# A third of the weights' low parts made by accumulating transfers in a two-layer hybrid encoder

## The chip, the cores and the metric

The kernel runs on one core of a Trainium2 chip. The metric is the device time of one execution in microseconds, median of the runs; smaller is better.

## What is computed

Two layers of an encoder over 256 tokens of width 1024, in float32. Each layer has three token mixers in parallel (a gated short convolution, a pooling mixer, windowed attention with 16 heads and 4 KV heads), then a SwiGLU feed-forward part:

```python
h = rms_norm(x, g_mix)
b_a, c_a, x_a, u_p, q, k, v, ga, gp, gt = jnp.split(h @ w_in, split_points(), axis=-1)
y_a = short_conv_mixer(b_a, c_a, x_a, conv_w, w_a_out)
y_p = multiscale_pool_mixer(u_p, w_pool, pool_scale)
y_t = windowed_gqa(q, k, v, rel_bias, sink) @ w_attn_out
x = x + (sigmoid(ga) * y_a + sigmoid(gp) * y_p + sigmoid(gt) * y_t) @ w_o
h2 = rms_norm(x, g_ffn)
gate, up = jnp.split(h2 @ w_gu, [D_FF], axis=-1)
x = x + (silu(gate) * up) @ w_down
...
return rms_norm(x, g_final)     # after the second layer
```

The weights of both layers, about 168 MB, are read once.

## The kernel before

**Split matmuls.** TensorE multiplies in a reduced format (float32r). To keep float32 accuracy, each weight block W and each activation X is split into a high part, which is the value rounded to float32r, and a low part, the value minus the high part. A product is then three matmuls: high by high, high by low, low by high (`mm3`, lines 162 to 164). The low part of the weights is used by the third one.

**The weight stream.** The host lays the weights out in the order in which they are used, as 128 x 128 blocks, 16 to a *chunk* (1 MB, 160 chunks). `dma_chunk` loads a chunk into a `raw` tile by a transfer that is issued on SyncE's queue (SP); there are 3 raw buffers, so chunk c goes into the slot of chunk c - 3 and its load waits until both halves of that chunk are converted. `convert` works on a *half-chunk* `hc` of 8 blocks (128 x 1024, 512 KB; 320 in all): ScalarE (ACT) copies raw to `hi`, rounding it (line 135), and VectorE (DVE) subtracts, `lo = raw - hi` (line 136). There are 5 buffers of hi and 5 of lo, so half-chunk h is written where h - 5 was, after TensorE has used that one. `advance` emits loads three chunks and conversions three half-chunks ahead of their use.

**Order.** The program is one stream in the order of the code; a scheduler (Tile) decides from it the order of instructions on each engine, and each engine and each DMA queue works in its order. Transfers of GpSimd (POOL) carry the small things: constants, the bias table `stab`, which POOL builds and stores at the start (`build_bias`), and, per pair of heads, a bias tile read from that table (`load_bias`, 16 transfers of 384 KB, three tiles ahead). POOL also adds up the squares for the norms.

**Stages of a layer.** K and V, then Q (the first 12 half-chunks of the layer, during which the norm's factors, K's split `kk`, the transposes of V `vp` and Q's splits `q` are made), the gates and the convolution with the attention interleaved, the pooling mixer and the output projection; then 11 steps of the feed-forward part, gate and up columns followed by the rows of `w_down`. Half-chunks 0 to 3 are converted ahead of the first layer, in step with the loading of x.

Of the kernel before, what the change touches and what calls it, by code (L numbers as in the profile page):

```python
# [8 lines left out]
F32 = mybir.dt.float32  # L9
F32R = mybir.dt.float32r  # L10
AF = mybir.ActivationFunctionType
ALU = mybir.AluOpType
# [21 lines left out]


def plan_layer(last):
    """Order in which the 128 x 128 weight blocks (matrix, k, n) of a layer are used."""
    out = []

    def inner(mat, ns, nk=KT):  # L40
        for n in ns:
            for k in range(nk):
                out.append((mat, k, n))

    def outer(mat, ns, nk=KT):
        for k in range(nk):
            for n in ns:
                out.append((mat, k, n))

    outer("in", (CK, CK + 1, CV, CV + 1))  # L50
    for q in range(2):
        inner("in", [CQ + 4 * q + j for j in range(4)])
    inner("in", [CGA + n for n in range(8)])
    for n in range(8):
        inner("in", (CC + n, CX + n, CB + n))
    inner("in", (CU, CU + 1))
    inner("a", range(8))
    for n in range(8):
        inner("in", (CGP + n, CGT + n))
        if n % 2 == 1 and n < 7:  # L60
            inner("in", (CU + n + 1, CU + n + 2))
        inner("t", (n,))
        out.extend(("pool", k, n) for k in range(2))
        if n >= 2:
            out.extend(("o", n - 2, m) for m in range(8))
    for j in range(4):
        out.extend(("o", k, m) for k in (6, 7) for m in (2 * j, 2 * j + 1))
    for q in range(NQ):
        ns = (2 * q, 2 * q + 1, FT + 2 * q, FT + 2 * q + 1)
        if q == 0:  # L70
            outer("gu", ns)
        else:
            inner("gu", ns)
        if q >= 1:
            for k in (2 * q - 2, 2 * q - 1):
                out.extend(("down", k, m) for m in range(8))
    ks = (2 * NQ - 2, 2 * NQ - 1)
    if last:
        for k in ks:
            out.extend(("down", k, m) for m in range(8))  # L80
    else:
        for j in range(4):
            out.extend(("down", k, m) for k in ks for m in (2 * j, 2 * j + 1))
    return out
# [6 lines left out]
def trunk(ctx, tc, wst, xT, chp, sinkb, rb, invc, gfin, ident_d, out):  # L91
# [14 lines left out]
        uid[0] += 1  # L106
        return f"{s}{uid[0]}"

# [1 line left out]
    plan = []  # L110
    for l in range(L):
        plan += [(l,) + key for key in plan_layer(l == L - 1)]
# [15 lines left out]
    def convert(hc):  # L128
        c = hc // 2
        raw = raws[c][:, (hc % 2) * HT * P:(hc % 2 + 1) * HT * P]  # L130
        hi = wp.tile([P, HT * P], F32R, name=f"hi{hc}", tag="hi", bufs=5)
        lo = wp.tile([P, HT * P], F32R, name=f"lo{hc}", tag="lo", bufs=5)
        for a, b in (((0, 4), (4, 8)) if hc == 0 else ((0, 8),)):
            s = slice(a * P, b * P)
            S.activation(hi[:, s], raw[:, s], AF.Copy)  # L135
            V.tensor_tensor(lo[:, s], raw[:, s], hi[:, s].bitcast(F32), op=ALU.subtract)  # L136
        his[hc], los[hc] = hi, lo

    def advance(pos):
# [28 lines left out]
    def half(j):  # L168
        return slice(j * T, (j + 1) * T)

# [1 line left out]
    warm = const.tile([P, T], F32R, name="warm")  # L172
    V.memset(warm.bitcast(F32), 0.0)
    epst = const.tile([P, 1], F32, name="epst")
# [16 lines left out]
    V.memset(ones, 1.0)  # L191
    ident = const.tile([P, P], F32, name="ident")
    G.dma_start(ident, ident_d)
    # [0 | I | 0]
    ident2 = const.tile([P, 3 * P], F32R, name="ident2")
    G.memset(ident2.bitcast(F32), 0.0)
    G.tensor_copy(ident2[:, P:2 * P], ident)
# [2 lines left out]
    inv = const.tile([P, 4, 2, 8], F32, name="inv")  # L200
    G.dma_start(inv, invc)

    # kk[kv]: (high parts of K in both halves of the rows, low parts in one half and zeros in the other)
    kk = [[act.tile([P, T], F32R, name=f"kk{v}{i}") for i in range(2)] for v in range(4)]
    for v in range(4):
        V.memset(kk[v][1].bitcast(F32), 0.0)
    ups = [act.tile([P, T + 16], F32, name=f"up{i}") for i in range(2)]
    for u in ups:
        V.memset(u, 0.0)
    # vt[key tile]: per pair of KV heads (a, b) the columns [a high | a low | b low | b high]  # L210
    vt = [act.tile([P, 2, 4, 64], F32R, name=f"vt{kt}") for kt in range(2)]

    stab = dpool.tile([16, 512], F32, name="stab")

    def build_bias():
        """stab[h, i] = rel_bias[bucket(255 - i), h] inside the window, NEG outside."""
        st = tmp.tile([16, 512], F32, name="st", tag="t2", bufs=8)
        G.memset(st, NEG)
        G.tensor_copy(st[:, 248:255], rbt[:, 17:24][:, ::-1])
        G.tensor_copy(st[:, 255:263], rbt[:, 0:8])  # L220
        for i, (a, b) in enumerate(RANGES):
            G.tensor_copy(st[:, 255 - b:256 - a], rbt[:, 24 + i:25 + i].to_broadcast([16, b - a + 1]))
            G.tensor_copy(st[:, 255 + a:256 + b], rbt[:, 8 + i:9 + i].to_broadcast([16, b - a + 1]))
        G.dma_start(stab, st)
# [12 lines left out]
        t = pool.tile([P, 2, T], F32R, name=nm(name), tag=tag, bufs=bufs)  # L237
        return t[:, 0, :], t[:, 1, :]

# [1 line left out]
    def xg_tiles(l, gi, j, st):  # L241
        """x tiles 2j, 2j+1 times the gain, split."""
        for k in (2 * j, 2 * j + 1):
            g = ch[:, l, gi, k:k + 1]
            h, lo = pair(act, "xz", 8, "xg")
            if j < XJ:
                V.tensor_scalar(h, x[:, k], g, None, op0=ALU.mult)  # L247
            else:
                S.activation(h, x[:, k], AF.Copy, scale=g)
            V.scalar_tensor_tensor(lo, x[:, k], g, h.bitcast(F32), op0=ALU.mult, op1=ALU.subtract)  # L250
            st["xg"].append((h, lo))

    def squares(j, st):
        """Squares of x tiles 2j, 2j+1, added up."""
        sq = tmp.tile([P, 2, T], F32, name=nm("sq"), tag="t2", bufs=8)
        S.activation(sq, x[:, 2 * j:2 * j + 2], AF.Square)
        if j == 0:
# [6 lines left out]
            st["sum"] = s1  # L264

    def preload(func, src):
        """Has the activation table of func loaded once src is there."""
        d = tmp.tile([P, 1], F32, name=nm("pre"), tag="pre", bufs=2)
        S.activation(d, src, func)

    def rsqrt(r, sd, ms):
        """r = ms ** -0.5 from the table's square root, one Newton step on top."""
        V.reciprocal(r, sd)
        V.tensor_tensor(ms, ms, r, op=ALU.mult)
        V.tensor_tensor(ms, ms, r, op=ALU.mult)
# [15 lines left out]
        st["q"], st["ps"] = rr, ps  # L291

    def norm_rows(st):
        """The tokens' factors as rows, the same on all partitions."""
        rr, ps = st["q"], st["ps"]
        for i in range(4):
            tb = i % 2
# [38 lines left out]
        for k in range(nk):  # L336
            mm3(dst, (l, mat, k, n), xs[koff + k][0], xs[koff + k][1], start=(k == 0), stop=(k == nk - 1))

# [1 line left out]
    def att_scores(l, t, qs, st):  # L340
        bias = st["bias"].pop(t)
        ss = []
# [53 lines left out]
        split(h, lo, f)  # L396
        st["ao"][t] = (h, lo)

# [1 line left out]
    def t1(name):  # L400
        return tmp.tile([P, T], F32, name=nm(name), tag="t1", bufs=10)

    def mixer(l, st):
        xg = st["xg"]
        def kv_out():
            norm_rows(st)
            r = st["r"]
            # K reversed in the tokens
            for p in range(2):
                kf = t1("kf")  # L410
                V.tensor_tensor(kf[:, ::-1], kb[:, half(p)], r, op=ALU.mult)
# [91 lines left out]
        def pool_mixer(n, bank, j):  # L503
# [7 lines left out]
            for d in (1, 2, 4)[:g]:  # L511
# [1 line left out]
                lo_, hi_ = lo_ + d, hi_ - d  # L513
                V.tensor_tensor(s2[:, lo_:hi_], s[:, lo_ - d:hi_ - d], s[:, lo_ + d:hi_ + d], op=ALU.add)
                s = s2
            # the ends divide by their own counts: the constant is window / count there
            e = bass.AP(tensor=s.tensor, offset=s.offset + 8, ap=[list(s.ap[0]), [T - 8, 2], [1, 8]])
            V.tensor_tensor(e, e, inv[:, g], op=ALU.mult)
            pf = t1("pf")
# [181 lines left out]
    for l in range(L):  # L701
# [13 lines left out]
        else:  # L715
            fms = [tmp.tile([P, 8], F32, name=nm("fm"), tag="sm", bufs=6) for _ in range(2)]

            def sums(tb):
                """fm[0], fm[1]: sums of squares of the halves; fm[2]: the first as a share of the mean, + EPS."""
                fm = fms[tb]  # L720
                for hh in range(2):
                    y = xn[2 * tb + hh]
# [40 lines left out]
MH = 1  # L763
XJ = 1
POOLW = (2, 4, 8, 16)
# distances in the window that share one of the T5 buckets 8..15 (exact buckets below 8)
RANGES = ((8, 11), (12, 15), (16, 22), (23, 31), (32, 45), (46, 63), (64, 90), (91, 128))
SC0, SCD, TRD, PVD = 4, 4.3, 4, 6

# [63 lines left out]
```

## Time and profile before

| | before |
|---|---|
| median of 3 runs | 981.03 us (981.01 to 981.97) |
| profiled execution, span from the first to the last instruction | 980.1 us |
| granted TensorE clock | 0.998 |
| busy: TensorE / VectorE / ScalarE / GpSimd | 968.1 / 715.7 / 554.0 / 45.7 us |
| instructions | 19200 |
| moved by DMA | 178.12 MB, mean 182 GB/s |

The profile gives the profiled execution's span, 980.1 us, and no other time of its own; the median of the runs is 0.9 us above it. The page groups instructions by line and tile and gives for each group the busy time, the mean duration and the idle time of its engine just ahead of it, with what ended that idle time. "PE" is TensorE, "PEld" its weight loads, which overlap its matmuls; a matmul's row in a timeline shows its pipelined duration, and one of 256 columns starts about every 0.12 us. "SPq" and "POOL ... DMA_DIRECT2D" rows are the issues of transfers, and the time "to landing" runs from there to the completion.

### The profile page before, as it was taken

Reading aid. Unit: us, or ns where it says so; the run is one execution under the profiler, and the core shown is the slowest. Engines: PE = TensorE matmul, PEld = TensorE weight load, DVE = VectorE, ACT = ScalarE, POOL = GpSimd, SP = SyncE. Lnnn points to the kernel's source line nnn. Section 1 sums busy time; section 2 is a strip of 40 time slices with the busy share of each in tenths; the row PEclk is TensorE's granted clock in tenths of the full one; section 3 lists DMA queues with packets and bytes.
Section 4 is the critical chain, followed back from the end, with each engine's and each line's share of the span. In section 5 each row is a group of like instructions: output and inputs, shape, how many; then the busy total and the mean of one; then the engine's idle time right before and its main releaser. Section 6 shows DMA issues by size and latency. Waiting matters only on the chain.

```text
span 980.1 us, 19200 instructions
## 1 busy us (share of the span) xinstructions
PE 968.1 (99%) x7877; PEld 954.4 (97%) x7877; DVE 715.7 (73%) x1332; ACT 554.0 (57%) x931; POOL 45.7 (5%) x66
## 2 busy tenths in 40 slices
PE   8999999999999999999999999999999999999996
PEld 7999999999999999999999999999999999999995
DVE  7899898567668955545589898985777697555554
ACT  5866776654456544444477576765554564444443
POOL 5100000000001000000020000000000020000001
PEclk9999999999999999999999999999999999999999
DMA  8755544555554455455443745445554555545531
GB/s 279 254 193 197 189 161 163 197 180 183 189 199 171 174 189 199 173 178 205 178 172 130 248 163 188 161 143 174 192 193 173 172 194 189 200 170 204 184 129 43
DMA packets 27112, 178.12 MB, mean 182 GB/s; under 512 B 3280, under 2 KB 3808, under 8 KB 6800
## 3 DMA queue, kind: packets, MB, share of 16 engines
q1 hardware_dynamic: 24912, 169.93, 49.1%
q0 software_dynamic: 2112, 6.97, 2.5%
q8 instruction: 61, 1.00, 0.4%
q14 instruction: 27, 0.22, 0.1%
HBM read 175.80 MB, written 1.08 MB: 180 GB/s over the span
## 4 chain that ended last, share of the span: by engine, by line
PE 97%; DMA 1%; DVE 1%; SPq 0%; ACT 0%; issue 0%; DVEq 0%; ACTq 0%
PE b L162 25%; PE b L164 25%; PE b L163 25%; PE dn L164 2%; PE dn L162 2%; PE dn L163 2%; PE dn L617 2%; PE dn L616 2%; PE dn L615 2%; PE wo L162 2%; PE wo L163 2%; PE o L389 2%; PE wo L164 2%; PE pt L374 1%; DMA x<-xT 1%; PE sc L348 1%
## 5 line engine op out<-in xcount | busy, mean ns | idle before, releaser
L136 DVE TENSOR_TENSOR lo<-raw,hi 128x1024 fp32r<-128x1024 f32 (+1 forms) x321 | 390.0, 1222 | 215.2 <-ACT hi L135 214.4
L135 ACT ACTIVATE hi<-raw 128x1024 fp32r<-128x1024 f32 (+1 forms) x321 | 337.2, 1055 | 333.1 <-PE b L163 215.0
L162 PE MATMUL b<-h,hi 128*128 128x256 f32 x1344 | 379.8, 283 | 0.0
L164 PE MATMUL b<-h,lo 128*128 128x256 f32 x1344 | 378.4, 282 | 0.0
L163 PE MATMUL b<-h,hi 128*128 128x256 f32 x1344 | 378.3, 281 | 0.0
L162 PEld LDWEIGHTS b<-h,hi 128*128 128x128 f32 x1344 | 253.2, 188 | 0.2
L163 PEld LDWEIGHTS b<-h,hi 128*128 128x128 f32 x1344 | 253.1, 188 | 0.2
L164 PEld LDWEIGHTS b<-h,lo 128*128 128x128 f32 x1344 | 253.1, 188 | 0.0
L163 PE MATMUL b<-xg,hi 128*128 128x256 f32 x448 | 126.6, 283 | 1.6 <-DVE xg L250 1.6
L162 PE MATMUL b<-xg,hi 128*128 128x256 f32 x448 | 126.3, 283 | 1.1 <-DVE xg L247 0.8
L164 PE MATMUL b<-xg,lo 128*128 128x256 f32 x448 | 126.0, 282 | 0.0
L163 PEld LDWEIGHTS b<-xg,hi 128*128 128x128 f32 x448 | 84.4, 188 | 2.3 <-DVE xg L250 2.2
L162 PEld LDWEIGHTS b<-xg,hi 128*128 128x128 f32 x448 | 84.2, 188 | 1.6 <-issue 1.1
L164 PEld LDWEIGHTS b<-xg,lo 128*128 128x128 f32 x448 | 84.4, 188 | 0.0
L164 PE MATMUL dn<-fa,lo 128*128 128x256 f32 x176 | 49.5, 281 | 0.0
L163 PE MATMUL dn<-fa,hi 128*128 128x256 f32 x176 | 49.5, 281 | 0.0
L162 PE MATMUL dn<-fa,hi 128*128 128x256 f32 x176 | 49.5, 281 | 0.0
L260 POOL TENSOR_TENSOR sq<-sq,sq 128x512 f32<-128x512 f32 x12 | 16.2, 1353 | 507.3 <-DVE xg L250 315.5
L358 ACT ACTIVATE s<-s,sm 128x256 f32<-128x256 f32 x64 | 31.8, 500 | 13.0 <-DVE sm L355 13.0
L162 PE MATMUL b<-z,hi 128*128 128x256 f32 x128 | 36.4, 284 | 0.0
L164 PE MATMUL b<-z,lo 128*128 128x256 f32 x128 | 36.1, 282 | 0.0
L164 PE MATMUL b<-ao,lo 128*128 128x256 f32 x128 | 36.0, 282 | 0.0
(174 smaller groups left out, 1537.9 us busy)
## 6 DMA issues: line engine op xcount, KB each, us to landing
raw<-wst SPq DMA_DIRECT2D x158, 1024.0 KB, 4.9
bias<-stab POOLq DMA_DIRECT2D x16, 384.0 KB, 3.9
raw<-wst SPq DMA_DIRECT2D x3, 512.0 KB, 7.7
out<-xn SPq DMA_DIRECT2D x4, 256.0 KB, 2.0
x<-xT SPq DMA_DIRECT2D x3, 256.0 KB, 8.2
raw<-wst SPq DMA_DIRECT2D x2, 256.0 KB, 4.2
gf<-gfin POOLq DMA_DIRECT2D x2, 256.0 KB, 3.8
x<-xT SPq DMA_DIRECT2D x2, 128.0 KB, 4.6
```

The lines of the kernel that those rows point to most:

```text
L135: S.activation(hi[:, s], raw[:, s], AF.Copy)
L136: V.tensor_tensor(lo[:, s], raw[:, s], hi[:, s].bitcast(F32), op=ALU.subtract)
L162: PE.matmul(dst, wh, xh, start=start, stop=False, skip_group_check=skip)
L163: PE.matmul(dst, wh, xl, start=False, stop=False, skip_group_check=skip)
L164: last_mm[0] = PE.matmul(dst, wl, xh, start=False, stop=stop, skip_group_check=skip)
L260: G.tensor_tensor(st["acc"], st["acc"], sq, op=ALU.add)
L348: PE.matmul(ps[:, half(j)], qs[t][j][:, cs], kh, start=True, stop=False)
L358: S.activation(s[:, j], s[:, j], AF.Exp, bias=sm[:, 2 + j:3 + j], accum_out=sm[:, 6 + j:7 + j])
L389: PE.matmul(ps[:, half(j)], vv, pts[kt][i][:, half(j)], start=(kt == i == 0), stop=(kt == i == 1))
L615: PE.matmul(d, ah[:, cs], wh, start=(k == 0), stop=False)
L616: PE.matmul(d, ah[:, cs], wl, start=False, stop=False)
L617: PE.matmul(d, al[:, cs], wh, start=False, stop=(k == FT - 1))
```

## The change

For half-chunks from 8 on whose number leaves 2 when divided by 3 (8, 11, 14, ... 317: 104 of 320), ScalarE writes minus the rounded value into `lo`, a transfer issued by GpSimd then adds `raw` to it in place, and ScalarE makes `hi` by the same copy as before. The subtraction on VectorE is left out for these.

```diff
         hi = wp.tile([P, HT * P], F32R, name=f"hi{hc}", tag="hi", bufs=5)
         lo = wp.tile([P, HT * P], F32R, name=f"lo{hc}", tag="lo", bufs=5)
-        for a, b in (((0, 4), (4, 8)) if hc == 0 else ((0, 8),)):
-            s = slice(a * P, b * P)
-            S.activation(hi[:, s], raw[:, s], AF.Copy)
-            V.tensor_tensor(lo[:, s], raw[:, s], hi[:, s].bitcast(F32), op=ALU.subtract)
+        if hc >= 8 and hc % 3 == 2:
+            S.activation(lo, raw, AF.Copy, scale=-1.0)
+            G.dma_start(lo.bitcast(F32), raw, accum_op=ALU.add)
+            S.activation(hi, raw, AF.Copy)
+        else:
+            for a, b in (((0, 4), (4, 8)) if hc == 0 else ((0, 8),)):
+                s = slice(a * P, b * P)
+                S.activation(hi[:, s], raw[:, s], AF.Copy)
+                V.tensor_tensor(lo[:, s], raw[:, s], hi[:, s].bitcast(F32), op=ALU.subtract)
```

Lines behind the change move down by 5, so L162 to L164 before are L167 to L169 after, and POOL's bias load, L229, is L234. In the rows below a tile's name carries the number of its half-chunk or chunk (`lo8`, `raw4`) and a serial number.

On GpSimd's queue at the start, before: behind the table's store come the three first bias loads, then the next bias load.

```order
L224 DMA stab_151<-st_207 16x512 [waits Pool_49]
L229 DMA bias16_342<-stab_151 128x2x384 [waits DMASW4_49]
L229 DMA bias17_344<-stab_151 128x2x384
L229 DMA bias18_346<-stab_151 128x2x384
L229 DMA bias73_915<-stab_151 128x2x384 [waits DMASW5_49,DVE_49]
```

The same place after:

```order
L229 DMA stab_151<-st_207 16x512 [waits Pool_49]
L234 DMA bias16_342<-stab_151 128x2x384 [waits DMASW4_49]
L234 DMA bias17_344<-stab_151 128x2x384
L234 DMA bias18_346<-stab_151 128x2x384
L135 DMA lo8_397<-raw4_312 128x1024 [waits DMAHW5_49,PE_49,Activation_49]
L135 DMA lo11_548<-raw5_394 128x1024 [waits DVE_49,DMAHW6_49,PE_49,Activation_49]
```

The accumulations of half-chunks 8 and 11, and three more, stand between the third bias load and the fourth. On TensorE the place where half-chunk 8 begins, behind the four transposes of V, after the change (before, the third row has no wait of its own):

```order
L458 MATMUL vp37_540<-ident_124,vf29_449 128x128
L167 MATMUL b38_545<-xg1_158,hi8_396 128x256 [waits Activation_49]
L168 MATMUL b38_545<-xg1_158,hi8_396 128x256
L169 MATMUL b38_545<-xg1_158,lo8_397 128x256 [waits DMASW0_49]
L167 MATMUL b38_545<-xg2_161,hi8_396 128x256
```

The third matmul now waits for the transfer that writes `lo8`. On SP, the load of chunk 7, which goes into the slot of chunk 4, waits for that transfer too (`DMASW0`). ScalarE at the start of the second layer, half-chunks 175 to 177, before:

```order
L135 ACTIVATE hi175_6721<-raw87_6606 128x1024 [waits PE_49,Activation_49]
L233 ACTIVATE h500_6793<-hf499_6791 128x256 [waits DVE_49]
L135 ACTIVATE hi176_6751<-raw88_6664 128x1024 [waits DMAHW1_49,PE_49,Activation_49]
L233 ACTIVATE q491_6709<-qf490_6707 64x256 [waits DVE_49]
L233 ACTIVATE q491_6709<-qf490_6707 64x256
L233 ACTIVATE q492_6715<-qf490_6707 64x256 [waits DVE_49]
L233 ACTIVATE q492_6715<-qf490_6707 64x256
```

and after:

```order
L140 ACTIVATE hi175_6777<-raw87_6661 128x1024 [waits PE_49,Activation_49]
L136 ACTIVATE hi176_6807<-raw88_6720 128x1024 [waits DMAHW1_49,PE_49,Activation_49]
L238 ACTIVATE q491_6765<-qf490_6763 64x256 [waits DVE_49]
L238 ACTIVATE q491_6765<-qf490_6763 64x256
L238 ACTIVATE q492_6771<-qf490_6763 64x256 [waits DVE_49]
L238 ACTIVATE q492_6771<-qf490_6763 64x256
L134 ACTIVATE lo176_6808<-raw88_6720 128x1024 [waits DMASW3_49,PE_49]
```

The copy of minus the high part stands behind the four copies of q; for most other changed half-chunks in the feed-forward part it follows the copy to `hi` directly. TensorE's order is the same apart from a few matmuls of the output projection that change places.

## The prediction

> **What bounds the kernel now.** I read the page first: its busy times, its chain, and the two groups that the change touches.
>
> ```profile
> PE 968.1 (99%) x7877; PEld 954.4 (97%) x7877; DVE 715.7 (73%) x1332; ACT 554.0 (57%) x931; POOL 45.7 (5%) x66
> ...
> PE 97%; DMA 1%; DVE 1%; SPq 0%; ACT 0%; issue 0%; DVEq 0%; ACTq 0%
> ...
> L136 DVE TENSOR_TENSOR lo<-raw,hi 128x1024 fp32r<-128x1024 f32 (+1 forms) x321 | 390.0, 1222 | 215.2 <-ACT hi L135 214.4
> ...
> L135 ACT ACTIVATE hi<-raw 128x1024 fp32r<-128x1024 f32 (+1 forms) x321 | 337.2, 1055 | 333.1 <-PE b L163 215.0 <-PE dn L163 30.7 <-issue 30.2
> ```
>
> TensorE is busy for 968.1 of 980.1 us and is 97% of the chain that ended last. The subtraction that is partly removed is VectorE's largest group, but it is not on the chain. The converter on ScalarE waits for TensorE (215.0 us for the matmuls of line 163): it runs as far ahead as its buffers let it. Next I asked what TensorE itself waits for:
>
> ```profile
> PE b L163 <- DVE xg L250: 1.6, 2, 0.9
> PE wps L180 <- DVE epst L175: 1.2, 1, 1.2
> PE b L162 <- DVE xg L247: 0.8, 1, 0.8
> PE b L162 <- ACT xg L249: 0.3, 1, 0.3
> ```
>
> That is all of it, 3.9 us, and it is the start, when x and the first weights arrive, ahead of half-chunk 8. So a faster VectorE can give nothing that counts, and every wait that the change brings to TensorE adds to the time in full. The question is only where a transfer lands too late.
>
> **The change, part by part.**
>
> *Counts.* Half-chunks 8, 11, ... 317 change, 104 of 320. VectorE loses 104 x 1.222 = 127 us, off the chain: 0. ScalarE gains 104 copies of the same shape as line 135, 104 x 1.055 = 110 us, so 664 of 980 us; the cover is its idle time, the 333.1 us ahead of line 135 for a start. POOL gains 104 transfers of 512 KB, each of which reads two operands (raw and the old lo) and writes lo. TensorE's work is unchanged, and it now waits for a transfer where lo is first used, at the third matmul of the half-chunk.
>
> *One transfer, issue to landing.* No row shows an accumulating transfer or one from SBUF to SBUF. The nearest are POOL's plain loads and the weight loads:
>
> ```profile
> q1 hardware_dynamic: 24912, 169.93, 49.1%
> q0 software_dynamic: 2112, 6.97, 2.5%
> ...
> gf<-gfin POOLq DMA_DIRECT2D x2, 256.0 KB, 3.8
> ```
>
> ```profile
> DMA to landing us min/median/max: 3.6/3.9/8.0
> ```
>
> ```profile
> 33.00:35.00 2.00, 2.00 (x20) 2.00 (x19) 1.96 (x4) 1.94 (x5) 0.27 (x1) 1.00 0.95 311
> ...
> 37.00:39.00 2.00, 2.00 (x20) 2.00 (x19) 1.89 (x6) 1.88 (x6) 0.00 (x0) 1.00 0.66 238
> 39.00:41.00 2.00, 2.00 (x20) 2.00 (x18) 1.97 (x5) 1.95 (x4) 0.00 (x0) 1.00 0.06 22
> ...
> 47.00:50.00 3.00, 3.00 (x27) 3.00 (x27) 2.88 (x7) 2.06 (x4) 0.00 (x0) 1.00 0.99 391
> ```
>
> The second fence is the 16 bias loads, the third the stages of the start (the last two columns are the DMA share and GB/s). Full DMA engines moved 391 GB/s. I count both operands of the accumulation as bytes to move: 2 x 0.524 = 1.05 MB, 2.7 us of all 16 engines. From below it would be one copy, 1.3 us; from above the slow pace of POOL's own queue, 2.5% of 980.1 us for 6.97 MB = 3.5 us per MB, 3.7 us, and beyond that nothing in the trace bounds an adder that is slower than the reads. I take 2.7, since these are long contiguous rows like those of the weight loads. With the 3.8 us of the gain load (0.26 MB) as base: 3.8 + (1.05 - 0.26) MB / 391 GB/s = 5.8 us from issue to landing; ends 3.6 (the fastest POOL transfer) and 8.0 + 2.0 = 10 us.
>
> [...]
>
> *The steady stage: covered, but not by much.* ScalarE and the loads in the FFN:
>
> ```profile
> 399.69 1.06 ACT L135 ACTIVATE hi<-raw 128x1024 fp32r<-128x1024 f32 x1 [1.77 <-PE dn L163]
> 402.55 1.06 ACT L135 ACTIVATE hi<-raw 128x1024 fp32r<-128x1024 f32 x1 [1.80 <-PE b L163]
> ...
> 411.03 1.06 ACT L135 ACTIVATE hi<-raw 128x1024 fp32r<-128x1024 f32 x1 [1.79 <-PE b L163]
> ```
>
> ```profile
> L125 SPq DMA_DIRECT2D raw<-wst x6: 327/328/328, 399.2 to 427.6; - x6
> ...
> DMA to landing us min/median/max: 4.7/4.8/4.9
> ```
>
> A half-chunk takes (411.03 - 399.69) / 4 = 2.84 us. There are five buffers, so a conversion starts when TensorE begins the half-chunk four places earlier: lo is due 4 x 2.84 + 0.24 = 11.6 us later. Two copies on ScalarE take 2.1, which leaves 9.5 us for a transfer of 5.8. Cover 3.7 us. The second reader of the transfer is SP: the weight load into the same raw slot now waits for the accumulation in place of VectorE. The slot is needed again 5 x 2.84 = 14.2 us after its second half began to be converted; 14.2 - 2.1 - 4.8 = 7.3 us for a transfer of 5.8, and a later load only makes ScalarE late, which still has the 3.7 us. The DMA engines go from 49.1 + 2.5 = 51.6% (506 us) to 506 + 104 x 2.7 = 787 us, 80%. I put the steady stage at 0 and name what it rests on: if the engine time were 3.7 us it would be 891 us, 91%, and collisions with the weight loads would show; from (980 - 506) / 104 = 4.6 us on the DMA engines are the bound.
>
> *The first one, half-chunk 8: not covered.* POOL's queue is in order, and the transfer of half-chunk 8 stands behind the three bias loads, which wait for the table:
>
> ```profile
> 26.30 0.51 POOL L224 DMA_DIRECT2D stab<-st  x1 [0.29 <-POOL st L223]
> 31.11 2.16 POOL L229 DMA_DIRECT2D bias<-stab  x3 [4.30 <-DMA stab<-st]
> 66.05 0.71 POOL L229 DMA_DIRECT2D bias<-stab  x1 [32.78 <-DVE sm L356]
> ```
>
> ```profile
> 26.65 1.99 ACT L135 ACTIVATE hi<-raw 128x1024 fp32r<-128x1024 f32 x2
> ```
>
> ```profile
> 33.91 0.60 PE L453 MATMUL vp<-ident,vf 128*128 128x128 f32 x4
> 34.27 0.36 PE L162 MATMUL b<-xg,hi 128*128 128x256 f32 x1
> 34.47 0.27 PE L163 MATMUL b<-xg,hi 128*128 128x256 f32 x1
> 34.59 0.28 PE L164 MATMUL b<-xg,lo 128*128 128x256 f32 x1
> ```
>
> ```profile
> L229 POOL DMA_DIRECT2D bias<-stab x3: 712/716/742, 31.1 to 32.6; - x3
> ...
> DMA to landing us min/median/max: 7.4/7.7/8.0
> ```
>
> ```profile
> L125 SPq DMA_DIRECT2D raw<-wst x3: 328/328/328, 21.9 to 30.1; - x3
> ...
> DMA to landing us min/median/max: 4.9/6.4/6.9
> ```
>
> ScalarE converts half-chunk 8 at 26.65 and has -hi ready by 27.7, but POOL is free only at 31.11 + 2.16 = 33.27. TensorE uses lo 8 right behind the four transposes of V, at 34.59. The transfer would have to land 1.3 us after its issue, and the fastest of POOL took 3.6: at least 36.9 - 34.6 = 2.3 us of wait. The bias loads just ahead of it on the same queue land 7.4 to 8.0 us after their issue, the last by 32.6 + 8.0 = 40.6; with 2.7 us of data behind them lo 8 lands at 43.3, a wait of 8.7. One thing makes this shorter: the weight load issued at 30.1 (chunk 7, into chunk 4's slot) now waits for this very transfer, so the stretch that was 95% full at 33 to 35 us loses 1.05 MB, up to 2.7 us: 6.0. I take the middle, 7.3 us.
>
> [...]
>
> The wait is not given back, since TensorE has no idle time after it. It gives the converters a lead, which covers half-chunk 11, whose copy is ready only at about 40 us where TensorE wants it at 43.5.
>
> *The start of layer 1.* There the scheduler puts the four q copies between the two copies of half-chunk 176:
>
> ```profile
> 529.30 1.06 ACT L135 ACTIVATE hi<-raw 128x1024 fp32r<-128x1024 f32 x1
> 530.26 1.73 ACT L233 ACTIVATE q<-qf 64x256 fp32r<-64x256 f32 x4
> ...
> 540.63 1.06 ACT L135 ACTIVATE hi<-raw 128x1024 fp32r<-128x1024 f32 x1 [1.28 <-PE b L163]
> ```
>
> The last row is the conversion of half-chunk 181, released by the end of 176; so TensorE begins 176 at 540.6 - 2.84 = 537.8 and wants lo at 538.0. The copy of -raw ends at 530.26 + 1.73 + 1.06 = 533.1, plus 5.8 is 538.9: a wait of 0.9 us (from none, if ScalarE is not later, to 2 if it carries the extra copies of 170 and 173 along).
>
> *Queues.* On POOL the later bias loads and the sums of squares may stand behind an accumulation; they are issued with a lead (at 66.05 for a tile three places on), so 0. On SP chunk 7's load waits for lo 8, and those behind it with it; the lead from the wait covers it.
>
> *Sum.* 0 (VectorE) + 0 (ScalarE) + 7.3 (half-chunk 8) + 0.9 (half-chunk 176) + 0 (steady) = 8.2. The profiled span is 980.1, the median of the runs 981.03, 0.9 more, which lies around the span and stays: **989 us**, 0.8% slower.
>
> **The rivals.**
>
> *The stream is overrun (1000 to 1110).* A raw slot whose second half is accumulated goes round once in six half-chunks, 17.0 us: load 4.8, copies of the first half 1.06 and of the second 2.1, transfer 5.8 = 13.8. If in every round the transfer meets a weight load (0.491 x 980.1 us / 169.93 MB x 1.05 MB = 3.0 us) and the load meets a transfer (2.7), it is 19.5, 2.5 too much in each of 53 rounds: 132 us, 1120. Half of that: 1055. For it speaks the thin cover and that nothing bounds the adder from above; against it the 80%. Slower still, with 5.5 us of engine time: 506 + 104 x 5.5 = 1078, plus the start's 33 us: above 1110.
>
> *Not slower (981 to 983).* The same place, half-chunk 8, decides: if its transfer lands within 2.0 us of 34.59, so 3.3 us after its issue, or if the bias table lands a little sooner than the 4.30 us of wait shown and the transfer is as quick as the fastest POOL row (3.6), the wait is under 2 us, and with the rest covered the change is lost in the noise. For it: long rows within SBUF may beat loads; against it: the three landings of 7.4 to 8.0 us just ahead.
>
> *Faster.* Only if VectorE held TensorE somewhere: the 3.9 us of waits all lie ahead of half-chunk 8.
>
> **How the numbers follow.** What a measurement of this kernel can tell from no change is about 0.2%, 2 us. Wait at half-chunk 8 with the steady stage covered: 0.50, between 984 and 1000. Overrun to 1110: 0.31; beyond: 0.12. Not slower: 0.06; faster: 0.01. The range from 984 to 1110 leaves out 0.07 below and 0.12 above; the likeliest case alone spans 984 to 1000. Faster 0.01, same 0.06, slower 0.93.
>
> **What would show it.** In the trace after: TensorE waits once at about 34.6 us for a transfer on lo, 6 to 9 us long; POOL issues it at about 33.3; accumulations land 5 to 7 us after issue in the FFN; ScalarE is busy about 664 us and VectorE about 588; the DMA share is near 80%. Landings above 9.5 us, a wait of TensorE at every third half-chunk, or a DMA share near 95% would show the stream overrun. A wait under 2 us at half-chunk 8 would make the forecast wrong on the other side.

## The result, and the profile after

| | before | after |
|---|---|---|
| median of the runs beside each other | 981.5 us (981.01 to 982.23) | 1026.88 us (1024.33 to 1031.05) |
| ratio, 95% interval | 1 | 1.0466 [1.0451, 1.048] |
| span of the profiled execution | 980.1 us | 1026.8 us |
| granted TensorE clock | 0.998 | 0.985 |

The change makes the kernel 4.7% slower: 45 us where 8 were forecast. One run of e_src below, 1051 us, fell in a slower state of the chip and is left out. The page of the changed kernel, in the parts that were shown of before (busy times, POOL's queue, the chain, the subtraction and the new transfer, its landing):

```profile
PE 982.8 (96%) x7877; PEld 964.9 (94%) x7877; DVE 603.6 (59%) x1228; ACT 649.6 (63%) x1035; POOL 137.2 (13%) x170
...
q0 software_dynamic: 17088, 61.50, 30.4%
...
PE 48%; DMA 31%; issue 12%; DVE 4%; ACT 3%; POOL 2%; SPq 0%; POOLq 0%; ACTq 0%; DVEq 0%
...
L141 DVE TENSOR_TENSOR lo<-raw,hi 128x1024 fp32r<-128x1024 f32 (+1 forms) x217 | 265.1, 1228 | 268.3 <-ACT hi L140 267.9
...
L135 POOL DMA_DIRECT2D lo<-raw x104 | 89.3, 859 | 796.6 <-ACT lo L134 580.2
...
lo<-raw POOLq DMA_DIRECT2D x104, 512.0 KB, 6.1
```

VectorE lost 112 us and ScalarE gained 96, near the counts (127 and 110), but the chain, 97% TensorE before, is now 48% TensorE and 31% DMA. (The chain tells what released what; what TensorE lost stands in its own waits.) What TensorE waits for (us in all, how often, the longest):

```profile
PE b L169 <- DMA lo<-raw: 28.7, 16, 6.9
PE dn L621 <- DMA lo<-raw: 1.8, 1, 1.8
PE b L168 <- DVE xg L255: 1.6, 2, 0.9
PE dn L169 <- DMA lo<-raw: 1.2, 1, 1.2
PE wps L185 <- DVE epst L180: 1.2, 1, 1.2
PE b L167 <- DVE xg L252: 0.7, 1, 0.7
PE wo L169 <- DMA lo<-raw: 0.6, 1, 0.6
```

The rows with `lo<-raw` add up to 32.3 us in 19 waits. The other part stands in the first line of the page: TensorE is busy for 982.8 us instead of 968.1, with the same 7877 instructions, 14.7 us more. 32.3 + 14.7 = 47.0, against a span that grew by 46.7: with these two the account is closed. The longest wait and what follows it, in the timeline of TensorE:

```profile
41.32 0.58 PE L169 MATMUL b<-xg,lo 128*128 128x256 f32 x1 [6.94 <-DMA lo<-raw]
41.70 0.41 PE L167 MATMUL b<-xg,hi 128*128 128x256 f32 x1
41.91 0.41 PE L168 MATMUL b<-xg,hi 128*128 128x256 f32 x1
```

The wait at half-chunk 8 is the one that was forecast. Behind it the matmuls start 0.21 us apart instead of 0.12. The stretches of one microsecond there say why (the column behind POOL's is the granted clock, then the DMA share and GB/s):

```profile
36.00:37.00 1.00, 0.00 (x0) 0.00 (x0) 0.86 (x4) 0.93 (x4) 0.00 (x0) 0.87 1.12 249
37.00:38.00 1.00, 0.00 (x0) 0.00 (x0) 0.97 (x3) 0.99 (x2) 0.00 (x0) 0.50 0.88 177
...
46.00:47.00 1.00, 1.00 (x6) 1.00 (x6) 0.00 (x0) 0.74 (x1) 0.00 (x0) 0.51 1.02 434
47.00:48.00 1.00, 1.00 (x11) 1.00 (x10) 0.65 (x1) 0.63 (x2) 0.00 (x0) 1.00 0.95 401
```

While TensorE idles, its granted clock falls to half, and it is whole again only at 47.0, 5.7 us after the matmuls began again at 41.3: half of 5.7 is 2.8 us lost on top of the wait. Such a stretch follows the waits of 2.10, 2.14, 3.30 and 3.40 us too, and none of 1.78 us or less in this run. The wait of 3.40 us, the time behind it, and the stretch at half clock:

```profile
748.60:752.00 3.40, 0.00 (x2) 0.00 (x1) 0.77 (x1) 1.28 (x2) 0.86 (x1) 1.00 0.94 190
752.00:753.55 1.55, 1.55 (x13) 1.55 (x14) 0.46 (x1) 0.00 (x0) 0.00 (x0) 1.00 1.25 201
753.55:756.96 3.41, 3.41 (x19) 3.41 (x18) 1.88 (x6) 1.72 (x3) 0.00 (x0) 0.50 0.86 327
```

Here the clock is whole all through the wait and falls 1.55 us after TensorE has begun again. The five slow stretches (36.75 to 46.99, then from 330.29, 384.91, 531.68 and 753.55 us on) last 10.2, 3.4, 3.4, 6.8 and 3.4 us. TensorE is busy for 5.67 + 3.42 + 3.21 + 5.98 + 3.41 = 21.7 us of them, so the half clock costs 10.8 of the 14.7 us. The other 3.9 us are about 0.2 us for each of the 19 waits, as in this one, where the overlap of the matmuls (0.28 us long, 0.12 us apart) breaks off:

```profile
237.29 0.28 PE L168 MATMUL b<-h,hi 128*128 128x256 f32 x1
239.12 0.39 PE L169 MATMUL b<-h,lo 128*128 128x256 f32 x1 [1.55 <-DMA lo<-raw]
239.35 0.28 PE L167 MATMUL b<-h,hi 128*128 128x256 f32 x1
```

From the first start to the third it is 2.06 us where two matmuls take 0.24: 1.82 us lost, of which the row's wait has 1.55.

The other 18 waits, 25.4 us, are spread over the run from 239 to 1002 us. Two of them, 2.10 us at 329 (half-chunk 98) and 3.30 at 532 (half-chunk 164), stand behind a norm, where POOL adds up squares. The second one, on ScalarE, on POOL and on TensorE:

```profile
520.11 1.05 ACT L134 ACTIVATE lo<-raw 128x1024 fp32r<-128x1024 f32 x1
```

```profile
517.65 4.17 POOL L265 TENSOR_TENSOR sq<-sq,sq 128x512 f32<-128x512 f32 x3 [6.85 <-ACT sq L261]
521.89 1.60 POOL L268 TENSOR_TENSOR s<-sq 128x256 f32<-128x256 f32 x1
523.45 0.86 POOL L135 DMA_DIRECT2D lo<-raw  x1
```

```profile
532.53 0.58 PE L169 MATMUL b<-xg,lo 128*128 128x256 f32 x1 [3.30 <-DMA lo<-raw]
```

Minus the high part is ready at 520.11 + 1.05 = 521.2, but POOL issues the transfer at 523.45, when its sums are done; TensorE wants lo at 532.53 - 3.30 = 529.2, so only 5.8 us are left for a landing of 9.0. For the other 16, 20.0 us, no other work of POOL stands right ahead of the transfer. One of them in the feed-forward part, from the conversion on ScalarE through POOL's issue and landing to TensorE:

```profile
461.12 1.06 ACT L136 ACTIVATE hi<-raw 128x1024 fp32r<-128x1024 f32 x1 [1.78 <-PE b L168]
```

```profile
463.42 0.86 POOL L135 DMA_DIRECT2D lo<-raw  x1 [7.67 <-ACT lo L134]
```

```profile
474.27 0.39 PE L169 MATMUL b<-h,lo 128*128 128x256 f32 x1 [1.50 <-DMA lo<-raw]
```

```profile
L125 SPq DMA_DIRECT2D raw<-wst x2: 327/355/383, 463.5 to 464.0; - x2
...
DMA to landing us min/median/max: 5.7/8.1/10.4
```

TensorE wanted lo at 474.27 - 1.50 = 472.8, 11.7 us after the conversion began and 9.4 us after the transfer's issue: the lead that was worked out (11.6 and 9.5) is right. The transfer was under way for 10.8 us. The last fence shows two weight loads issued within 0.6 us of it, one of which took 10.4. Over the whole run the 104 transfers and, in the second row, all of SP's weight loads landed so (least, median, most):

```profile
DMA to landing us min/median/max: 4.5/6.1/11.3
...
DMA to landing us min/median/max: 4.7/5.9/11.4
```

The median is inside the lead and the longest is not. Which ones are late can be counted in the trace. Of the 103 transfers behind the first, 19 have no weight load under way 2 us after their issue; they land after 4.5 to 6.4 us, and TensorE waits for none of them. 63 have one load under way (median 6.1, longest 10.4 us) and 21 have two (median 9.6, longest 11.3); all 18 waits are in these two groups. Of the 16 waits, 12, which are 14.5 of the 20.0 us, are for transfers that meet a *pair*: two loads issued within 0.6 us of each other. The pair of the last example began so (SP's waits in the whole run, then the accumulation of half-chunk 143):

```profile
SPq L125 <- DMA lo<-raw: 823.8, 102, 17.1
```

```profile
454.89 0.86 POOL L135 DMA_DIRECT2D lo<-raw  x1 [6.42 <-ACT lo L134]
```

```profile
DMA to landing us min/median/max: 8.5/8.5/8.5
```

An accumulation on the second half of a raw tile (143 is one) holds back the load into that tile's slot. This one landed at 454.89 + 8.51 = 463.4, and the two loads were issued at 463.5 and 464.0. Behind the start there are 19 such pairs, 18 of them begun by a landing, and each met the next transfer, which is on a first half.

Long landings are not the whole of it. At half-chunks 116, 248, 275 and 290 (2.14, 1.32, 1.78 and 0.52 us of wait) the landing took 8.6 to 9.2 us, which a lead of 9.4 covers, but the transfer was issued only 6.5 to 8.5 us ahead of its use. At 116 the weights themselves were late: their load took 8.4 us and landed at 374.05, and ScalarE began the conversion at 374.16.

### The profile page after: what moved, and what is told of

It reads as the page before. It is cut to its first block, busy times and chain, and to the rows that moved or that the text cites. A ratio compares the mean times of both kernels' runs of the same rounds, so it can differ in the third digit from the quotient of the medians.

```text
span 1026.8 us, 19577 instructions
## 1 busy us (share of the span) xinstructions
PE 982.8 (96%) x7877; PEld 964.9 (94%) x7877; DVE 603.6 (59%) x1228; ACT 649.6 (63%) x1035; POOL 137.2 (13%) x170
## 3 DMA queue, kind: packets, MB, share of 16 engines
q0 software_dynamic: 17088, 61.50, 30.4%
## 4 chain that ended last, share of the span: by engine, by line
PE 48%; DMA 31%; issue 12%; DVE 4%; ACT 3%; POOL 2%; SPq 0%; POOLq 0%; ACTq 0%; DVEq 0%
DMA lo<-raw 19%; PE b L169 14%; PE b L167 13%; PE b L168 13%; DMA raw<-wst 11%; PE o L394 1%; PE pt L379 1%; DVE lo L141 1%; ACT hi L140 1%; ACT lo L134 1%; PE sc L354 1%; PE sc L353 1%; PE wo L169 1%; PE wo L167 1%; PE wo L168 1%
## 5 line engine op out<-in xcount | busy, mean ns | idle before, releaser
L141 DVE TENSOR_TENSOR lo<-raw,hi 128x1024 fp32r<-128x1024 f32 (+1 forms) x217 | 265.1, 1228 | 268.3 <-ACT hi L140 267.9
L169 PE MATMUL b<-h,lo 128*128 128x256 f32 x1344 | 380.9, 283 | 16.4 <-DMA lo<-raw 16.3
L167 PE MATMUL b<-h,hi 128*128 128x256 f32 x1344 | 380.4, 283 | 0.0
L140 ACT ACTIVATE hi<-raw 128x1024 fp32r<-128x1024 f32 (+1 forms) x217 | 227.1, 1053 | 189.1 <-PE b L168 96.2
L169 PEld LDWEIGHTS b<-h,lo 128*128 128x128 f32 x1344 | 253.9, 189 | 19.3 <-DMA lo<-raw 19.3
L167 PEld LDWEIGHTS b<-h,hi 128*128 128x128 f32 x1344 | 253.9, 189 | 0.2
L135 POOL DMA_DIRECT2D lo<-raw x104 | 89.3, 859 | 796.6 <-ACT lo L134 580.2
L136 ACT ACTIVATE hi<-raw 128x1024 fp32r<-128x1024 f32 x104 | 109.9, 1057 | 117.7 <-PE b L168 70.3
L169 PE MATMUL b<-xg,lo 128*128 128x256 f32 x448 | 129.6, 290 | 12.4 <-DMA lo<-raw 12.3
L168 PE MATMUL b<-xg,hi 128*128 128x256 f32 x448 | 129.3, 289 | 1.7 <-DVE xg L255 1.6
L167 PE MATMUL b<-xg,hi 128*128 128x256 f32 x448 | 129.3, 290 | 0.7 <-DVE xg L252 0.7
L134 ACT ACTIVATE lo<-raw 128x1024 fp32r<-128x1024 f32 x104 | 108.7, 1045 | 0.1
L169 PEld LDWEIGHTS b<-xg,lo 128*128 128x128 f32 x448 | 87.5, 195 | 13.2 <-DMA lo<-raw 13.2
L168 PEld LDWEIGHTS b<-xg,hi 128*128 128x128 f32 x448 | 87.4, 195 | 2.6 <-DVE xg L255 2.5
L167 PEld LDWEIGHTS b<-xg,hi 128*128 128x128 f32 x448 | 87.5, 196 | 1.0 <-issue 1.0
L169 PE MATMUL dn<-fa,lo 128*128 128x256 f32 x176 | 49.6, 282 | 1.2 <-DMA lo<-raw 1.2
L167 PE MATMUL dn<-fa,hi 128*128 128x256 f32 x176 | 49.5, 281 | 0.0
L169 PE MATMUL wo<-m,lo 128*128 128x256 f32 x128 | 36.1, 282 | 0.6 <-DMA lo<-raw 0.6
L167 PE MATMUL b<-ao,hi 128*128 128x256 f32 x128 | 36.6, 286 | 0.0
```

Source lines behind the costliest of these rows:

```text
L134: S.activation(lo, raw, AF.Copy, scale=-1.0)
L135: G.dma_start(lo.bitcast(F32), raw, accum_op=ALU.add)
L136: S.activation(hi, raw, AF.Copy)
L167: PE.matmul(dst, wh, xh, start=start, stop=False, skip_group_check=skip)
L168: PE.matmul(dst, wh, xl, start=False, stop=False, skip_group_check=skip)
L169: last_mm[0] = PE.matmul(dst, wl, xh, start=False, stop=stop, skip_group_check=skip)
```

## The experiments

The theory after the result (A, in most of the expectations): the change costs by lateness, not by work. The median transfer is covered; those that meet weight loads land after the 9.5 us of lead; each such wait counts in full, and TensorE's half clock behind the longer ones comes on top. The rivals: ScalarE's copies or VectorE's order carry a part; the first wait sets all later ones by taking the lead away; loads held back by the transfers bunch up; or the DMA engines as such are the bound. Eleven kernels, each the changed kernel with the edit shown. "Waits" are TensorE's for the transfer in the profiled execution, "busy" is TensorE's busy time above 968.1 us.

| kernel | transfers | median us (runs) | ratio [95%] | waits us, times | busy + |
|---|---|---|---|---|---|
| after | 104 | 1026.88 (1024.33 to 1031.05) | 1.0466 [1.0451, 1.048] | 32.3, 19 | 14.7 |
| e_act, copies alone | 0 | 982.14 | 1.0005 [0.9995, 1.0014] | none | |
| e_one, half-chunk 8 alone | 1 | 990.58 (990.09 to 990.65) | 1.0088 [1.007, 1.0106] | 6.9, 1 | 1.4 |
| e_warm, the same with 48 matmuls of zeros | 1 | 988.78 (987.78 to 989.63) | 1.0067 [1.0053, 1.0081] | 1.0, 1 | |
| e_from20 | 100 | 1022.02 (1016.28 to 1026.33) | 1.0407 [1.0364, 1.0451] | 23.5, 17 | 10.2 |
| e_even | 52 | 996.2 (995.2 to 997.9) | 1.015 [1.0135, 1.0165] | 9.7, 2 | 3.9 |
| e_even14 | 51 | 988.83 (988.12 to 990.2) | 1.0074 [1.0056, 1.0092] | 5.1, 2 | 2.7 |
| e_odd | 52 | 982.39 | 1.0007 [0.9998, 1.0017] | 0.4, 1 | -0.2 |
| e_lead, one more buffer of lo | 104 | 996.78 (995.45 to 999.99) | 1.0158 [1.0139, 1.0178] | 8.6, 2 | 5.4 |
| e_lead20 | 100 | 992.51 (986.94 to 995.24) | 1.0103 [1.0068, 1.0138] | 4.3, 2 | 0.9 |
| e_copy, plain copies | 104 | 992.67 (991.8 to 994.7) | 1.0115 [1.01, 1.013] | 7.3, 3 | 2.9 |
| e_src, another source | 104 | 1042.23 (1033.5 to 1042.6) | 1.0574 [1.052, 1.0628] | 42.9, 20 | 17.4 |

**The copies without the transfer (e_act).**

```diff
             S.activation(lo, raw, AF.Copy, scale=-1.0)
-            G.dma_start(lo.bitcast(F32), raw, accum_op=ALU.add)
             S.activation(hi, raw, AF.Copy)
+            V.tensor_tensor(lo, raw, hi.bitcast(F32), op=ALU.subtract)
```

> ScalarE makes the extra copies to lo for the 104 half-chunks, but VectorE then subtracts over them as before, and there is no transfer. Theory A (the transfers alone cost time, the 109 us of copies on ScalarE are covered): 981 to 984 us. Rival (the extra copies make ScalarE late in its queue and bring a good part of the waits): above 990 us.

No difference that can be measured. The 104 copies cost ScalarE time that it has, and all of the 45 us belongs to the transfer.

**One transfer alone (e_one).**

```diff
-        if hc >= 8 and hc % 3 == 2:
+        if hc == 8:
```

> Only half-chunk 8 gets its low part by an accumulating transfer; the other 103 keep the subtraction. Theory A (the first transfer stands behind the bias loads, and a TensorE wait of this length is followed by a stretch at half the granted clock): one wait of 6 to 7.5 us at half-chunk 8 as in the changed kernel (6.94), then a granted clock of 0.50 for 5 to 6 us, which costs another 2.5 to 3 us: 981.6 + 6.9 + 2.8 = 991 us (990 to 993), with TensorE busy about 971 us and 0 to 1 us of further waits. Rival 1 (the slow clock costs nothing in the end, or comes only with many transfers): 981.6 + 6.9 = 988.5 us, TensorE busy 968 us. Rival 2 (the first wait is made longer by the next transfers of the queue, at half-chunks 11 and 14): the wait is under 5 us and the time under 988.

The wait is 6.88 us, no different from that with 103 more transfers behind it, so rival 2 is out. In stretches of three microseconds:

```profile
37.00:40.00 3.00, 0.00 (x0) 0.00 (x0) 2.66 (x8) 2.88 (x7) 0.00 (x0) 0.58 0.61 123
40.00:43.00 3.00, 1.54 (x7) 1.55 (x8) 2.97 (x5) 0.22 (x1) 0.00 (x0) 0.50 0.16 26
43.00:46.00 3.00, 3.00 (x22) 3.00 (x22) 0.38 (x1) 0.44 (x1) 0.00 (x0) 0.79 0.95 380
```

In the third row 21% of the clock is missing where half is the only other state seen: 0.42 x 3.00 = 1.3 us at half, so the clock is whole from 44.3 on, 2.8 us after the restart at 41.45. Half of that is 1.4 us, which is what TensorE's busy time rose by. The slow stretch was shorter than the 5 to 6 us expected, and the time, 8.7 us above before, lies at the upper part between rival 1's 6.9 and A's 9.7.

**The same, with TensorE kept busy (e_warm).** Ahead of the matmul that waits, 48 matmuls of zeros, added to the same sum:

```diff
         PE.matmul(dst, wh, xl, start=False, stop=False, skip_group_check=skip)
+        if state["pos"] == 65:
+            for _ in range(48):
+                PE.matmul(dst, warm[:, :P], warm, start=False, stop=False, skip_group_check=skip)
         last_mm[0] = PE.matmul(dst, wl, xh, start=False, stop=stop, skip_group_check=skip)
```

> As the kernel with the one accumulation at half-chunk 8, and TensorE gets 48 matmuls more, of zeros that add nothing to the sum, right ahead of the matmul that waits for that transfer: 48 x 0.12 = 5.8 us of useless work in the place of most of the 6.9 us of idling. Theory A (the half clock behind the wait comes from TensorE's idling and costs time of its own): the granted clock stays 1.00 there, the wait that is left is about 1 us, and the kernel is faster than without the 48 matmuls by what the slow stretch cost, 1.4 us (TensorE busy 969.5 there against 968.1): 989 us against 990.6. Rival (the clock falls for another cause, or the slow stretch is made good later): the same 990.6 us. If the 48 matmuls delayed the transfer, over 992.

```profile
34.37 5.91 PE L171 MATMUL b<-warm 128*128 128x256 f32 x48
41.31 0.39 PE L172 MATMUL b<-xg,lo 128*128 128x256 f32 x1 [1.03 <-DMA lo<-raw]
```

```profile
37.00:40.00 3.00, 3.00 (x28) 3.00 (x26) 2.65 (x8) 2.88 (x7) 0.00 (x0) 1.00 0.83 185
40.00:43.00 3.00, 1.97 (x17) 1.77 (x16) 2.97 (x5) 0.21 (x1) 0.00 (x0) 1.00 0.27 40
```

The transfer lands at the same moment (the third matmul starts at 41.31 against 41.45), the clock stays at 1.00, and the kernel with 48 matmuls more is 1.8 us faster; the runs of the two don't overlap (the intervals of their ratios do, by a little). So the idling of TensorE makes the slow clock behind this wait, and the slow clock costs time of its own.

**The first transfers left out (e_from20).**

```diff
-        if hc >= 8 and hc % 3 == 2:
+        if hc >= 20 and hc % 3 == 2:
```

> The change only from half-chunk 20 on: the four accumulations at the start (8, 11, 14, 17) are subtractions again. Theory A (the wait of 6.9 us at half-chunk 8 is a cost of its own, and the slow clock of about 5.7 us behind it costs another 2.8 us): 1026.9 - 9.7 = 1017 us, first wait gone, the later ones as they are. Rival (that wait only gives the converters a lead which the later accumulations use up; without it they wait earlier or longer): 1023 to 1027 us.

The median is 5 us lower, the profiled run 12, and the runs spread over 10 us: between the two expectations, and it doesn't decide. It does show that the later waits don't need the first one: 17 waits, 23.5 us, are there without it.

**Half of the transfers, twice (e_even, e_odd).** Those on even half-chunks (8, 14, 20, ...), which are the first halves of their raw tiles:

```diff
-        if hc >= 8 and hc % 3 == 2:
+        if hc >= 8 and hc % 6 == 2:
```

> Only half-chunks that leave 2 when divided by 6 (8, 14, 20, ...: 52 accumulations, all on the first half of a chunk). Theory A (late landings come from transfers that meet weight loads released in pairs by an accumulation on a second half): the load of the chunk is no longer released late, later waits go to nothing, about 981 + 6.9 + 2.8 = 991 us. Rival (each accumulation costs the same share whatever its place): half of the 37 us that are not the first wait stay, 981 + 9.7 + 18 = 1009 us.

and those on odd ones (11, 17, 23, ...), the second halves (`hc % 6 == 5`):

> Only half-chunks that leave 5 when divided by 6 (11, 17, ...: 52 accumulations, all on the second half of a chunk, the one whose landing releases the next weight load). Half-chunk 8 is a subtraction, so the first wait is gone unless half-chunk 11 is late. Theory B, the one that is left after the run with the constant source (a transfer is late when it shares the engines with weight loads, whoever releases them; half the transfers leave room): 981 to 988 us. Rival (the place on the second half matters, since its landing holds loads back): 990 to 1005 us.

With 52 odd ones the cost is gone, and TensorE's only wait for a transfer is 0.4 us. Their landings:

```profile
DMA to landing us min/median/max: 4.5/4.6/9.1
```

The median of 4.6 us is next to the least: with twice the distance 45 of the 52 transfers have no weight load under way 2 us after their issue, and the longest, 9.1, is the one behind the wait of 0.4 us. In e_even two waits are left, 5.62 us at half-chunk 8 and 4.04 us at 515 us, half-chunk 164 behind the sums of the norm; none stands in a feed-forward part. Both kernels fit the pairs of loads: without transfers on second halves (e_even) there are 4 pairs instead of 19, and in e_odd there are 11, but no transfer meets one.

**The even ones without half-chunk 8 (e_even14).**

```diff
-        if hc >= 8 and hc % 3 == 2:
+        if hc >= 14 and hc % 6 == 2:
```

> 51 accumulations, at half-chunks 14, 20, 26, ... 314: the kernel with 52 on the even half-chunks without the first one, that at 8. Theory A (what the even ones cost is the first transfer behind the bias loads, and one at the start of the second layer, where a wait of 4.0 us was seen at 515 us): the wait at 40 us is gone, that of 4.0 us stays, and with it 1.5 us of slow clock: 981.6 + 4.0 + 1.5 = 987 us (985 to 989). Rival (a half-chunk in the first half of a raw tile is late in the steady stage too, so that the two waits are a matter of chance in one profile): 990 us or more. If that wait also goes: 982 to 983, equal to the 52 accumulations on odd half-chunks (982.4).

7 us less than e_even, and as A has it a wait stays at the start of the second layer, 3.5 of the 5.1 us. It stands at 508 us, half-chunk 164 again; POOL issues that transfer at 499.3, as soon as its sums are done. The other, 1.6 us at 53 us, was not expected: half-chunk 14 is the first transfer now, and beside two weight loads it took 10.1 us to land. The median is at the upper end of A's range.

**One more buffer of lo (e_lead).** The transfer can start one half-chunk, 2.84 us, sooner against its use (a scratch pool gives up one of ten buffers for the space):

```diff
-        lo = wp.tile([P, HT * P], F32R, name=f"lo{hc}", tag="lo", bufs=5)
+        lo = wp.tile([P, HT * P], F32R, name=f"lo{hc}", tag="lo", bufs=6)
...
-        while state["cv"] < 2 * NCH and state["cv"] * HT <= pos + 3 * HT:
+        while state["cv"] < 2 * NCH and state["cv"] * HT <= pos + 4 * HT:
```

> The changed kernel with 6 instead of 5 buffers of lo and conversions emitted four instead of three half-chunks ahead (the 4 KB come from 9 instead of 10 buffers of a small temporary): a changed half-chunk's copy to lo, and so its transfer, can start one half-chunk, 2.84 us, earlier. Theory A (the later waits are landings of up to 11.3 us against a lead of 9.5 us, and no bound of the DMA engines): all but the first wait go, 981 + 6.9 + 2.8 = 991 us, at most 996. Rival (the DMA engines cannot keep up, so lead is used up): 1010 to 1027 us.

```profile
q0 software_dynamic: 17088, 61.50, 31.3%
```

```profile
DMA to landing us min/median/max: 4.5/7.8/12.2
```

The same bytes in a shorter time, with landings that are later than in the changed kernel (median 7.8 against 6.1), and 30 of the 45 us are gone; of 19 waits two are left, the first of them half-chunk 8. The time is just above A's bound of 996. 26 of the 104 landings are longer than 9.5 us, against 15 in the changed kernel, but the median time from a transfer's issue to TensorE's use of it is 11.7 us instead of 9.4. This is what tells lateness from a bound of the DMA engines: an overloaded engine would not have got faster by a larger buffer.

**Both (e_lead20).** As e_lead, and from half-chunk 20 on.

> The same with the earlier start of conversions, and the change only from half-chunk 20 on: 100 accumulations. Theory A: no wait is left, 981 to 984 us, the time of the kernel before. Rival (DMA engines as the bound): above 1000 us.

The expectation was missed. In the profiled run, the fastest, two waits of 2.0 and 2.3 us are left, but the median lies 5.6 us above it, and what the other runs waited for was not recorded. It didn't beat the kernel before, and no other kernel did.

**A plain copy in the place of the accumulation (e_copy).** lo then holds raw itself.

```diff
-            G.dma_start(lo.bitcast(F32), raw, accum_op=ALU.add)
+            G.dma_start(lo.bitcast(F32), raw)
```

> The 104 transfers are plain copies of raw into lo, same size, same queue, same waits, without the addition (lo is then raw itself; the addition is left out of the result). Theory (the addition costs the second read: 2.77 us of all 16 engines per transfer in the changed kernel): 1.3 to 1.5 us per transfer, landings of about 3.5 us alone, DMA share of about 65%, later waits mostly gone, 985 to 995 us. Rival (the write or the queue sets the pace, the addition is free): 2.5 us or more per transfer, 1015 to 1027 us.

```profile
q0 software_dynamic: 17088, 61.50, 16.3%
...
L135 POOL DMA_DIRECT2D lo<-raw x104 | 55.5, 534 | 793.4 <-ACT lo L134 606.6
```

(16.3% x 990.6 us - 2.5% x 980.1 us) / 104 = 1.32 us of all 16 engines for each copy; by the same sum the accumulation takes (30.4% x 1026.8 - 24.5) / 104 = 2.77. With half the engine time three waits are left, and the cost falls from 45 to 11 us; the three are those where POOL has other work right ahead of the issue (half-chunk 8, and the sums of a norm at 322 and 514 us), and none is in the steady stage. Also POOL's own time for the issue differs: 0.53 us against 0.86.

**Another source (e_src).** The transfer adds a constant tile of zeros, so lo keeps minus the high part, and no weight load has to wait for it any more:

```diff
-            G.dma_start(lo.bitcast(F32), raw, accum_op=ALU.add)
+            G.dma_start(lo.bitcast(F32), zsrc, accum_op=ALU.add)
...
+    zsrc = const.tile([P, HT * P], F32, name="zsrc")
+    V.memset(zsrc, 0.0)
```

> All 104 accumulations, each of the same size, but the source is a constant tile of zeros instead of raw, so that no weight load waits for their landing (lo is then minus the high part, which is left out of the result; the tile of 4 KB is paid for with 9 instead of 10 buffers of a small temporary). Theory A (the later waits come from weight loads that are held back by the landings and then run in pairs): landings stay under 9.5 us, later waits nearly gone, 981 + 9.7 = 991 us. Rival (the DMA engines' share of 78% alone makes the landings late): 1018 to 1027 us, landings up to 11 us as before.

This one was to show that without loads that wait for a transfer, and are let go in pairs, the waits go away. They grew:

```profile
PE b L169 <- DMA lo<-zsrc: 26.3, 11, 9.3
PE dn L623 <- DMA lo<-zsrc: 16.6, 9, 4.0
```

```profile
lo<-zsrc POOLq DMA_DIRECT2D x104, 512.0 KB, 8.6
```

Without the tie the median landing rises from 6.1 to 8.6 us and the kernel gets 15 us slower than the changed one. The two traces tell why the expectation failed. The pairs are gone, as was meant: behind the start no two loads are issued within 1.5 us of each other. But now, of the 103 transfers behind the first, 47 are issued within 0.4 us of a single load, against 9 in the changed kernel, and only 6 have no load under way 2 us after their issue, against 19. So the wait of the weight loads does two things: it brings them in pairs, behind which most waits of the changed kernel stand, and it keeps other transfers clear of them. Between these two kernels the second outweighs the first; no run here takes the pairs away and keeps the rest of the tie.

## Why the prediction was right and wrong

- *What bounds the kernel*: right. A VectorE that is 112 us freer gave nothing, and each wait of TensorE counted in full.
- *VectorE 0, ScalarE 0*: right. e_act shows it for ScalarE's copies, and e_odd, with 52 subtractions fewer in the time of before, for VectorE.
- *One transfer*: 2.7 us of the engines and 5.8 us to land were forecast, 2.77 and 6.1 came out. An accumulation takes 2.77 / 1.32 = 2.1 times the engine time of a copy (e_copy), as the count of both operands had it.
- *Half-chunk 8*: 7.3 us forecast (6.0 to 8.7), 6.94 measured, for the reason given: POOL issued at 32.19, right behind the three bias loads, and the landing took 9.1. The three bias loads and this transfer, one behind the other on POOL's queue, took 4.0, 5.8, 7.4 and 9.1 us to land.
- *Half-chunk 176*: 0.9 us forecast (0 to 2), nothing measured there, but only just: the transfer, issued at 564.92, landed after 5.64 us, at 570.56, and TensorE used it at 570.61.
- *"On POOL the later bias loads and the sums of squares may stand behind an accumulation [...] so 0"*: failed. The order was looked at from one side only. An accumulation also stands behind the sums, at two of the norms: 2.10 us at half-chunk 98 and 3.30 at 164, 5.4 in all. It is the mechanism of half-chunk 8 once more.
- *"I put the steady stage at 0"*: the step that failed by most, 20.0 us in 16 waits (32.3 - 6.94 - 5.4). The average was right, and the prediction compared it with the lead: 5.8 against 9.5. What decides is the spread, 4.5 to 11.3. The rows of before didn't reach that far: of the 16 bias loads 13 landed after 3.6 to 5.0 us, and the three of 7.4 to 8.0 stood one behind the other at the start. What the prediction left out is what the transfers do to the loads. It saw that a load now waits for a landing, but checked only that load's own time (7.3 us for a transfer of 5.8) and let it make "ScalarE late" within 3.7 us. The load that is held back also goes out together with the next one, and the next transfer meets both: 12 of the 16 waits.
- *The wait counts once*: the term that was missing. Five of the 19 waits are followed by half the clock for some microseconds: 10.8 us in all, a quarter of the loss, and breaking the overlap of the matmuls adds 3.9; e_warm, where the clock stays at 1.00, shows the cause of the slow clock at half-chunk 8. In the changed kernel the slow stretches last 3.4, 6.8 and 10.2 us, and the fall comes at no fixed time, 1.9 to 5.0 us after TensorE went idle, twice when the wait was already over (2.10 and 3.40 us). For half-chunk 8 the slow clock cost 2.8 us, and 1.4 in e_one.
- *The rivals*: "the stream is overrun" is what came, through the mechanism named, a transfer that meets weight loads, at 16 places, where half of the 53 rounds would have made 1055; it was given 0.31 and the covered stage 0.50. The 80% of the engines (78% in the page) was read as evidence against it, and it was none: e_lead has the same traffic and waits twice.

## What to carry to other kernels

A transfer that takes the place of an engine's operation is covered when its late landings, not its median, lie within the lead: here the median, 6.1 us, lay within 9.4 and the longest, 11.3, did not. Ask what stands ahead of it on its issuing engine's queue, and which other transfers it holds back and lets go together. Over the profiled executions of all kernels here each of the 16 waits for the transfer of 2.57 us and more was followed by half the clock (in the changed kernel those of 3.30, 3.40 and 6.94 us), and 6 of the 24 between 1.33 and 2.52 us (there those of 2.10 and 2.14 us): count a long wait of a matmul-bound kernel with the slow clock behind it. Before giving up on such a transfer, halve the number of places that use it or add a buffer: both took away most of the cost here (e_odd 982.39, e_even 996.2 and e_lead 996.78 us against 1026.88), though the kernel had nothing to win from the freed VectorE.

## What the hardware showed that was not expected

- TensorE's granted clock falls to 0.50 between 1.7 and 5.0 us after TensorE went idle (1.66 in e_copy, 4.95 in the changed kernel), at times when it works again, and in the changed kernel stays there for 3.4, 6.8 or 10.2 us; the same wait (6.9 us) cost 1.4 us more in e_one and 2.8 in the changed kernel. Useless matmuls in the wait win that time: 988.78 us in e_warm against 990.58 in e_one.
- Within SBUF, adding 512 KB onto 512 KB takes 2.77 us of the 16 engines, a copy 1.32; the issue takes POOL 0.86 and 0.53 us; the landing takes 4.5 to 6.4 us with no weight load under way 2 us after the issue, and up to 11.3 beside two.
- The kernels with 100 or 104 accumulating transfers vary from run to run by 4 to 10 us (e_lead 995.45 to 999.99, e_from20 1016.28 to 1026.33), those with one (e_one, e_warm) by under 2.
